# Gate scans behind the gate weight's split, and value-window copies spread between attention units, in a hybrid encoder layer

## The chip, the cores and the metric

The kernel runs on one core of a Trainium2 chip. The metric is the device time of one execution in microseconds (us). Differences are stated in us and, where it helps, in per cent of the 1353.88 us median of the kernel before.

## What is computed

One encoder layer over 1024 tokens of width 1024, with 16 learned meta tokens put in front. A normalised input `u` is multiplied by one wide weight `w_in`; the columns of the product feed two groups of heads:

```
u = rmsnorm(h);  q_na, k_na, v_na, q_gl, k_gl, v_gl, g_gl, z_gl = split(u @ w_in)
o_na = rmsnorm(neighbourhood_attention(q_na, k_na, v_na, rpb))
la   = log_sigmoid(z @ up + bias) / 16            (gates, forward and backward)
b    = cumsum(la) within chunks of 64             (the "gate scan")
o_gl = rmsnorm(gla(q*exp(b), k*exp(-b), v)) * silu(g_gl)
h    = h + rmsnorm([o_na, o_gl] @ w_o);  h = h + rmsnorm(conv_gated_ffn(rmsnorm(h)))
```

The 8 attention heads look at a window of 8 rows by 16 columns of a 64-wide token grid, plus the meta tokens. The 4 gated-linear-attention (GLA) heads work in chunks of 64.

## The kernel before

Every float32 product is done as three products of split operands: a weight or activation is copied to a rounded high part `hi` on ACT (L148) and its remainder `lo = src - hi` is computed on DVE (L149). The program text is unrolled; at build time a planner simulates the engines and fixes the order of the instructions on each engine. Its priority is the order of the program text (moved forward inside `high_priority`), and an instruction is placed when the simulation finds it ready. Two calls constrain it. `keep_in_program_order(x)` adds an edge (order of issue only) from `x` to the instruction that precedes it in the text on the same engine; `issue_after(ins)` adds such an edge to `ins` from everything that the block traces on that engine.

**First place of the change: gates.** The gate stage handles 4 heads. `gla_gate(hd)` makes gate logits on PE, `|x|` on ACT (L307) and `min(x,0)` on DVE (L308), then exp and log on ACT (L309, L310), a subtraction on POOL (L311), and two scans on DVE (L312 for the forward half, L313 for the backward half) into `C`. `gla_exp(hd)` copies the chunk ends (POOL, L322 to L325), subtracts (POOL, L326 and L327), and takes three exponentials on ACT: of the difference into `A` (L334), of `-C` into a new buffer `B` (L335) and of `C` in place (L336). The tag `gb` of the buffers `B` has two slots, shared by the gate stage's `gt_b` (which the scans read) and by `gla_exp`'s `B`; the latter pair stays in use until `gla_head` runs, so the `B` of heads 0 and 1 can be placed only when the scans of heads 2 and 3 have read theirs. `pv` (L188 to L190) are nine row blocks of the GLA value projection, evacuated at L193. `proj_g(blk)` multiplies `u` by gate weight block `wg0` or `wg1` (L175 to L177, weights stationary), per head in three token parts of 272, 256 and 512 columns, whose PSUM tiles come from a tag with two buffers (`ps_a`, shared with `pv` and all later projections), and evacuates each with a Silu on ACT (L290). The first Silu is pinned:

```python
x = nc.scalar.activation(mgl[:, hd, ...], ps[:, s0:n], AF.Silu)      # L290
if hd == 0 and ci == 0:
    tc.keep_in_program_order(x)
```

In the kernel before, the text runs: `gla_gate(3)`, `gla_exp(0)`, `gla_exp(1)`, `pv(5, 9)`, `proj_g(0)`, and `proj_g(0)` itself begins with the load and split of `wg0`. So the ACT instruction that precedes the first Silu in the text is the `hi` copy of `wg0`'s second half. Exp/log and Silu belong to different activation tables; a switch is an ACT_TABLE_LOAD.

**Second place: value windows.** The attention values are projected in two blocks of 256 columns (`half` 0 and 1) into `v_d` in DRAM. `v_windows(half)` then copies, DRAM to DRAM on the SP queue, for each of four row blocks `b` and four column windows `q`, the rows that unit (b, half) will need into `vw_d[b, half, q]`: one DMA (L498) for b = 0 and 1, and two (L500 for the meta row, L501 for the rest) for b = 2 and 3; 24 DMAs a half. For `half` 1 this stands in the step list in `v 1`, between the attention units `na b p` (row block b, pair p of heads).

```python
T1 = ("qk 3", "na 0 0", "na 0 1", "v 1", "na 1 0", "na 1 1")
T2 = ("na 0 2", "wg 1", "na 0 3", "gains", "w15", "nn 0", "wg 2", "na 1 2", ...)
```

A unit loads its query `qr` (L624), its keys `kt0` and `kt1` (L639, or L641 and L642 for b of 2 and 3) and, when p is even, four value windows `vt` (L557, four slots in all, each freed by the last value product L694 of the units that used it). Its score products are L670 to L672, the probabilities' transposes L688, their copy to SBUF on ACT L690 (`pT`). Between T1 and T2 the eight row blocks of `w_o` are loaded (`wor`, L734, three slots) and split into `wo` (L148, L149); `wg i`, `wn i` and `w15` are products with `w_o` (L763 to L767, L780); `gains` loads two gain rows (L862) and `post_a` loads `xr` (L811).

Of the kernel before, what the change touches and what calls it, by code (L numbers as in the profile page):

```python
# [8 lines left out]
F32 = mybir.dt.float32  # L9
# [4 lines left out]
ALU = mybir.AluOpType  # L14
# [16 lines left out]
QC0 = (0, 8, 24, 40)  # L31
QW = (24, 32, 32, 24)
QT = (0, 1, 1, 2)
BR0 = (0, 0, 4, 8)
BNR = (8, 11, 11, 8)
# [15 lines left out]
def _mask_offsets():  # L51
# [18 lines left out]
)  # L70
T1 = ("qk 3", "na 0 0", "na 0 1", "v 1", "na 1 0", "na 1 1")
T2 = (
# [3 lines left out]
)  # L76
T3 = (
    "wt 6", "wn 7", "ul 1", "ul 2", "wg 8", "ul 3", "ul 4", "ul 5", "u15", "wn 8", "fr", "wt 7",
# [4 lines left out]
def kernel(ctx: ExitStack, tc: tile.TileContext, a: dict):  # L83
    nc = tc.nc
# [10 lines left out]
    vw_d = {  # L95
        (b, half, q): dram.tile([(BNR[b] + 1) * QW[q], 256], F32, name=f"vw_d{b}_{half}_{q}")
        for b in range(4)
        for half in range(2)
        for q in range(4)
    }  # L100
# [36 lines left out]
    def col(i):  # L137
        return vec[:, i : i + 1]

    def rstd_small(pool, ss, n, width, name):  # L140
        v = pool.tile([P, 1], F32, tag="rs_v", name=f"{name}_v", bufs=6)
        r = pool.tile([P, 1], F32, tag="rs_r", name=f"{name}_r", bufs=6)
        nc.vector.tensor_scalar(v[:n], ss, 1.0 / width, EPS, ALU.mult, ALU.add)  # L143
        nc.gpsimd.tensor_tensor(r[:n], v[:n], nhalf[:n], ALU.pow)  # L144
        return r

    def split(hi, lo, src):
        nc.scalar.copy(hi, src)  # L148
        nc.vector.tensor_tensor(lo, src, hi.bitcast(F32), ALU.subtract)  # L149

    t1 = ExitStack()
    up = t1.enter_context(tc.tile_pool(name="up", bufs=1))
# [4 lines left out]
    def load_w(src, w, name):  # L157
        hs, ls = [], []
        for kh in range(2):
            raw = wp.tile([P, 4, 256], F32, tag="wr", name=f"{name}_r{kh}", bufs=2)  # L160
            nc.sync.dma_start(raw[:, :, :w], src[:, 4 * kh : 4 * kh + 4, :])
            hi = wp.tile([P, 4, 256], F32R, tag="wh", name=f"{name}_h{kh}")
            lo = wp.tile([P, 4, 256], F32R, tag="wl", name=f"{name}_l{kh}")
            split(hi[:, :, :w], lo[:, :, :w], raw[:, :, :w])
            hs.append(hi)
            ls.append(lo)
        return hs, ls
# [40 lines left out]
    with tc.tile_pool(name="p1", bufs=2) as p1:  # L208
        g_pre = p1.tile([P, D], F32, name="g_pre", bufs=1)
        nc.sync.dma_start(g_pre, a["norm_mix_pre"].broadcast_to([P, D]))  # L210
        for i in range(9):
            n = NM if i == 0 else P
# [6 lines left out]
            r = rstd_small(p1, ss[:n], n, D, f"rs1_{i}")  # L219
# [10 lines left out]
            if i == 1:  # L230
                vw = load_w(a["w_in_b"][4], 256, "wvg0")
# [7 lines left out]
    def gla_tile(tag, name, bufs):  # L239
        return gp.tile([P, L], F32, tag=tag, name=name, bufs=bufs)  # L240
# [39 lines left out]
        nc.gpsimd.memset(t, 0.0)  # L280
        asb.append(t)

    def proj_g(blk):
        hs, ls = load_w(a["w_in_b"][blk], 256, f"wg{blk}")
        for j in range(2):
            hd = 2 * blk + j

            def evac_g(ci, t0, n, ps, hd=hd):
                s0 = 15 if ci == 0 else 0
                x = nc.scalar.activation(mgl[:, hd, t0 + s0 - 15 : t0 + n - 15], ps[:, s0:n], AF.Silu)  # L290
                if hd == 0 and ci == 0:
                    tc.keep_in_program_order(x)

            proj_t(hs, ls, j * P, P, evac_g, f"pg{hd}")

    gA, gB, gC, gdec = {}, {}, {}, {}

    def gla_gate(hd):
        A = gla_tile("ga", f"gt_a{hd}", 2)
        B = gla_tile("gb", f"gt_b{hd}", 2)  # L300
        C = gp.tile([P, L], F32, name=f"gc{hd}")
        gbias = col(VEC_GB + hd)
        for ci, (t0, n) in enumerate(TOK):
            ps = (ps_s, ps_b, ps_c)[ci](f"gate{hd}_{ci}")
            mm(ps[:, :n], gwh[:, hd, :], zT[:, t0 : t0 + n], start=True, stop=False)
            mm(ps[:, :n], gwl[:64, hd, :], zT[:64, t0 : t0 + n], start=False, stop=True)
            nc.scalar.activation(A[:, t0 : t0 + n], ps[:, :n], AF.Abs, bias=gbias)  # L307
            nc.vector.tensor_scalar(B[:, t0 : t0 + n], ps[:, :n], gbias, 0.0, ALU.add, ALU.min)  # L308
        nc.scalar.activation(A, A, AF.Exp, scale=-1.0)  # L309
        nc.scalar.activation(A, A, AF.Ln, bias=1.0)  # L310
        nc.gpsimd.tensor_sub(B, B, A)  # L311
        nc.vector.tensor_tensor_scan(C[:64], d0[:64], B[:64], 0.0, ALU.mult, ALU.add)  # L312
        nc.vector.tensor_tensor_scan(C[64:, ::-1], d0[64:, ::-1], B[64:, ::-1], 0.0, ALU.mult, ALU.add)  # L313
        gC[hd] = C

    def gla_exp(hd):
        A = gla_tile("ga", f"ga{hd}", 2)
        B = gla_tile("gb", f"gb{hd}", 2)
        C = gC[hd]
        Cx = C[:, NM:].rearrange("p (n c) -> p n c", c=64)  # L320
        bl = gp.tile([P, 17], F32, tag="bl", name=f"bl{hd}", bufs=2)
        nc.gpsimd.tensor_copy(bl[:64, 0:1], C[:64, NM - 1 : NM])  # L322
        nc.gpsimd.tensor_copy(bl[64:, 0:1], C[64:, 0:1])
        nc.gpsimd.tensor_copy(bl[:64, 1:17], Cx[:64, :, 63])
        nc.gpsimd.tensor_copy(bl[64:, 1:17], Cx[64:, :, 0])  # L325
        nc.gpsimd.tensor_sub(A[:, :NM], bl[:, 0:1].broadcast_to([P, NM]), C[:, :NM])  # L326
        nc.gpsimd.tensor_sub(  # L327
            A[:, NM:].rearrange("p (n c) -> p n c", c=64),
            bl[:, 1:17].unsqueeze(2).broadcast_to([P, NCH, 64]),
            Cx,  # L330
        )
        dec = gp.tile([P, 17], F32, tag="dec", name=f"dec{hd}", bufs=2)
        nc.scalar.activation(dec, bl, AF.Exp, scale=0.0625)
        nc.scalar.activation(A, A, AF.Exp, scale=0.0625)  # L334
        nc.scalar.activation(B, C, AF.Exp, scale=-0.0625)  # L335
        nc.scalar.activation(C, C, AF.Exp, scale=0.0625)  # L336
        gA[hd], gB[hd], gdec[hd] = A, B, dec
# [143 lines left out]
    def na_v(half, after=None):  # L481
        hs, ls = load_w(a["w_in_b"][10 + half], 256, f"wvn{half}")
        for i in range(9):
            proj_v1(i, hs, ls, v_d, 256 * half, f"pvn{half}", True)
            if i == 0 and after is not None:
                after()
        v_windows(half)

    def v_windows(half):
        vv = v_d[:, 256 * half : 256 * half + 256].rearrange("(r c) d -> r c d", c=64)  # L490
        for b in range(4):
            nr, r0 = BNR[b], BR0[b]
            for q in range(4):
                w = QW[q]
                cols = slice(QC0[q], QC0[q] + w)
                dst = vw_d[b, half, q].rearrange("(r c) d -> r c d", c=w)
                if r0 == 0:
                    nc.sync.dma_start(dst, vv[: nr + 1, cols, :])  # L498
                else:
                    nc.sync.dma_start(dst[0], vv[0, cols, :])  # L500
                    nc.sync.dma_start(dst[1:], vv[r0 + 1 : r0 + 1 + nr, cols, :])  # L501

    hs, ls = load_w(a["w_in_b"][5], 256, "wvg1")
    pv = lambda i0, i1: [proj_v1(i, hs, ls, vg_d, 256, "pvg1") for i in range(i0, i1)]
    gla_gate(0)
    gla_gate(1)
    pv(0, 3)
    gla_gate(2)
    pv(3, 5)
    gla_gate(3)  # L510
    gla_exp(0)
    gla_exp(1)
    pv(5, 9)
    proj_g(0)
    proj_g(1)
    tc.keep_in_program_order(nc.scalar.preload_act_table_set("natural_log_exp_and_others"))
    steps = {"gqk": proj_qk, "head": gla_head, "exp": gla_exp, "qk": na_qk}

# [213 lines left out]
    for k in (4, 5, 6, 7, 0, 1, 2, 3):  # L732
# [3 lines left out]
        hi, lo = hl[:, :D], hl[:, D : 2 * D]  # L736
# [120 lines left out]
    gains = {}  # L857
# [8 lines left out]
    def nn(b):  # L866
        ms = ps_c(f"nms{b}")
        for t in range(2):
            mm(ms[:, t : t + 1], ssq[b][:, t * P : t * P + P], ones[:, :1], start=True, stop=True)
            rna[2 * b + t + 1] = rstd_small(pp3, ms[:, t : t + 1], P, 512, f"rna{b}_{t}")  # L870

    def step2(name):
        op, *n = name.split()
        n = [int(x) for x in n]
        if op == "na":
            na_step(*n)
        elif op == "nn":
            nn(*n)
        elif op == "gains":
            load_gains()  # L880
        elif op == "w15":
            wo_15()
        else:
            st = sts.setdefault(n[0] if n else 0, {})
            if op == "wg":
                wo_mm(n[0], st, 0)
            elif op == "wn":
                wo_mm(n[0], st, 1)
                post_a(n[0], st)
            elif op == "wt":  # L890
                post_b(n[0], st)
            elif op == "ul":
                u2_load(n[0])
            elif op == "u15":
                nc.gpsimd.tensor_copy(u2["a"][:, :, :1], u15)
            elif op == "fr":
                prep(0)
# [517 lines left out]
```

## Time and profile before

| | us |
|---|---|
| runs (median of 3) | 1353.88 (1353.38 to 1354.87) |
| the profiled execution, own time | 1352.37 |
| its span in the profile | 1350.7 |
| PE busy in the span | 1268.2 (94%) |
| DVE, ACT, POOL busy | 914.0, 619.3, 429.7 |

Mean granted TensorE clock over the span: 0.973 of full speed. The 1.67 us between the execution's own time and its span lie outside the traced instructions. "Idle" in a row is the time that the engine sat before an instruction, and the arrow names what ended that time; SPq rows are the issue of DMAs by the SP queue, not their transfer.

### The profile page before, as it was taken

What the parts mean: (1) busy time and instruction counts of PE and PEld (TensorE: products, weight loads), DVE (VectorE), ACT (ScalarE), POOL (GpSimd) and SP (SyncE); (2) the same over time, 40 slices, a digit from 0 to 9 for tenths busy, and PEclk for the clock granted to TensorE, in tenths of its full rate; (3) what the DMA queues carried; (4) which work ended last, traced back from release to release, by engine and by line L of the source; (5) the groups of instructions that cost most, each with busy time, mean ns of one, the idle gap of its engine ahead of it and who ended that gap; (6) DMA issues with size and microseconds to landing.
All of it is one profiled execution on the core that took longest, in us unless ns stands there. A gap on an engine that the chain in (4) does not pass through costs nothing.

```text
span 1350.7 us, 23581 instructions
## 1 busy us (share of the span) xinstructions
PE 1268.2 (94%) x9048; PEld 1139.0 (84%) x9050; DVE 914.0 (68%) x1453; ACT 619.3 (46%) x1198; POOL 429.7 (32%) x401
## 2 busy tenths in 40 slices
PE   7979999999997899998779999999999999999997
PEld 6869888988886587776779999999999998888876
DVE  6491365254544577865979898898888978555556
ACT  5443544152332555656544444344443444545542
POOL 1260001000021154432556565765657633000001
PEclk9989999999988889999889999999999999999999
DMA  6311132351187545842134434444344456866735
GB/s 204 119 38 50 34 93 84 110 177 64 51 270 225 208 132 197 278 137 94 40 117 149 142 124 164 167 154 143 124 164 159 154 173 228 303 198 207 247 125 187
DMA packets 117137, 203.74 MB, mean 151 GB/s; under 512 B 18080, under 2 KB 51200, under 8 KB 117024
## 3 DMA queue, kind: packets, MB, share of 16 engines
q1 hardware_dynamic: 117024, 202.24, 44.6%
q8 instruction: 71, 1.16, 0.4%
q14 instruction: 42, 0.34, 0.1%
HBM read 145.64 MB, written 66.19 MB: 157 GB/s over the span
## 4 chain that ended last, share of the span: by engine, by line
PE 63%; DVE 18%; DMA 6%; ACT 5%; issue 5%; POOL 1%; SPq 1%; DVEq 0%; ACTq 0%; POOLq 0%
DVE bl L924 5%; PE bank L1202 4%; PE bank L1201 4%; PE bank L1200 4%; PE q_r L966 3%; PE q_r L967 3%; PE q_r L968 3%; PE ops L694 2%; PE pna L175 2%; PE pna L176 2%; PE pna L177 2%; DVE g L1015 2%; PE pp L688 2%; PE wo L766 2%; PE wo L767 2%
## 5 line engine op out<-in xcount | busy, mean ns | idle before, releaser
L966 PE MATMUL q_r<-ah,bh 128*128 128x258 f32 x504 | 145.4, 288 | 14.9 <-ACT c L1079 14.9
L967 PE MATMUL q_r<-al,bh 128*128 128x258 f32 x504 | 144.3, 286 | 0.0
L968 PE MATMUL q_r<-ah,bl 128*128 128x258 f32 x504 | 143.9, 285 | 0.0
L966 PEld LDWEIGHTS q_r<-ah,bh 128*128 128x128 f32 x504 | 97.1, 193 | 17.2 <-ACT c L1079 17.1
L149 DVE TENSOR_TENSOR ol<-r,oh 128x512 fp32r<-128x512 f32 x116 | 74.6, 688 | 46.0 <-ACT oh L148 46.0
L1200 PE MATMUL bank<-oh,oh 128*128 128x512 f32 x264 | 102.9, 390 | 2.2 <-DVE c L1266 2.2
L1201 PE MATMUL bank<-oh,ol 128*128 128x512 f32 x264 | 102.7, 389 | 0.0
L1202 PE MATMUL bank<-ol,oh 128*128 128x512 f32 x264 | 102.2, 389 | 0.0
L966 PE MATMUL q_z<-ah,bh 128*128 128x258 f32 x336 | 95.4, 284 | 6.3 <-DVE y L1015 4.9
L1025 ACT ACTIVATE g<-g 128x512 f32<-128x512 f32 (+1 forms) x46 | 28.2, 614 | 157.0 <-DVE g L1015 156.9
L967 PEld LDWEIGHTS q_r<-al,bh 128*128 128x128 f32 x504 | 97.0, 193 | 0.0
L968 PEld LDWEIGHTS q_r<-ah,bl 128*128 128x128 f32 x504 | 97.0, 192 | 0.0
L967 PE MATMUL q_z<-al,bh 128*128 128x258 f32 x336 | 95.2, 283 | 0.0
L968 PE MATMUL q_z<-ah,bl 128*128 128x258 f32 x336 | 95.0, 283 | 0.0
L148 ACT CAST oh<-r 128x512 fp32r<-128x512 f32 x116 | 65.6, 619 | 50.2 <-PE bank L1201 40.0
L924 DVE TENSOR_TENSOR bl<-bt,bh 128x512 fp32r<-128x512 f32 x84 | 85.2, 1015 | 3.5 <-ACT bh L922 3.5
L924 DVE TENSOR_TENSOR bl<-fr,bh 128x512 fp32r<-128x512 f32 x67 | 64.5, 966 | 17.4 <-ACT bh L922 17.2
L1011 ACT ACTIVATE g<-c,vec 128x512 f32<-128x512 f32 (+1 forms) x46 | 36.6, 795 | 75.2 <-DVE c L1140 40.8
L966 PEld LDWEIGHTS q_z<-ah,bh 128*128 128x128 f32 x336 | 63.9, 190 | 6.7 <-issue 5.1
L144 POOL TENSOR_TENSOR rsc_r<-rsc_v,nhalf 128x1 f32<-128x1 f32 x8 | 5.8, 725 | 197.5 <-DVE rsc_v L143 197.5
L1014 DVE SCALAR_TENSOR_TENSOR g<-c,vec,g 128x512 f32<-128x512 f32 (+1 forms) x46 | 53.5, 1164 | 17.1 <-ACT g L1011 17.1
L1026 DVE TENSOR_TENSOR y<-y,g 128x512 f32<-128x512 f32 (+1 forms) x46 | 54.9, 1194 | 13.4 <-ACT g L1025 13.3
(388 smaller groups left out, 4257.9 us busy)
## 6 DMA issues: line engine op xcount, KB each, us to landing
fr<-in_w_ffn_in_dram SPq DMA_DIRECT2D x44, 512.0 KB
y_d<-y SPq DMA_DIRECT2D x44, 256.0 KB
w<-in_w_ffn_out_dram SPq DMA_DIRECT2D x22, 512.0 KB
t_d<-w SPq DMA_DIRECT2D x22, 512.0 KB
s_d<-y SPq DMA_DIRECT2D x44, 256.0 KB
r<-s_d SPq DMA_DIRECT2D x44, 256.0 KB
r<-t_d SPq DMA_DIRECT2D x44, 256.0 KB
r<-y_d SPq DMA_DIRECT2D x25, 256.0 KB
```

The costliest lines, as they stand in the source:

```text
L148: nc.scalar.copy(hi, src)
L149: nc.vector.tensor_tensor(lo, src, hi.bitcast(F32), ALU.subtract)
L924: nc.vector.tensor_tensor(lo, src, hi.bitcast(F32), ALU.subtract)
L966: mm(ps, w[0][:, k, :], A[0][:, k, c], start=(first and k == 0), stop=False, skip_group_check=True)
L967: mm(ps, w[0][:, k, :], A[1][:, k, c], start=False, stop=False, skip_group_check=True)
L968: mm(ps, w[1][:, k, :], A[0][:, k, c], start=False, stop=(last and k == 3), skip_group_check=True)
L1011: nc.scalar.activation(dst, tap(1), AF.Identity, bias=col(VEC_CB + ch), scale=col(VEC_CONV + 2 * NFC + ch))
L1014: nc.vector.scalar_tensor_tensor(dst, tap(0), col(VEC_CONV + ch), dst, ALU.mult, ALU.add)
L1026: nc.vector.tensor_mul(val, val, g)
L1200: mm(ps, A[0][:, tk], B[0], start=first, stop=False, skip_group_check=True)
L1201: mm(ps, A[1][:, tk], B[0], start=False, stop=False, skip_group_check=True)
L1202: mm(ps, A[0][:, tk], B[1], start=False, stop=last, skip_group_check=True)
```

## The change

The scans of heads 2 and 3 are taken out of `gla_gate` into `gla_scan` and stand in the text behind the load and split of `wg0`, with an order edge to the `lo` subtraction of `wg0`'s second half (`lo_last[0]`); `gla_exp(0)` and `gla_exp(1)` move behind them, and so behind `pv(5, 9)`. The load of `wg0` moves from inside `proj_g` to before the scans. The copies of value half 1 are split: b = 0 stays in `v 1`; b = 1, 2 and 3 become the steps `vw 1`, `vw 2`, `vw 3` behind `na 0 2`, `na 0 3` and `na 1 2`, each with an order edge to the last SP instruction that the text has at that point (the last DMA of that unit).

```diff
 T2 = (
-    "na 0 2", "wg 1", "na 0 3", "gains", "w15", "nn 0", "wg 2", "na 1 2", "wn 1", "na 1 3", "nn 1", "wt 1", "wn 2",
...
+    "na 0 2", "vw 1", "wg 1", "na 0 3", "vw 2", "gains", "w15", "nn 0", "wg 2", "na 1 2", "vw 3", "wn 1", "na 1 3",
...
     def split(hi, lo, src):
         nc.scalar.copy(hi, src)
-        nc.vector.tensor_tensor(lo, src, hi.bitcast(F32), ALU.subtract)
+        lo_last[0] = nc.vector.tensor_tensor(lo, src, hi.bitcast(F32), ALU.subtract).ins
...
-    def proj_g(blk):
-        hs, ls = load_w(a["w_in_b"][blk], 256, f"wg{blk}")
+    def proj_g(blk, w):
+        hs, ls = w
...
         nc.gpsimd.tensor_sub(B, B, A)
+        gB[hd], gC[hd] = B, C
+        if hd < 2:
+            gla_scan(hd)
+
+    def gla_scan(hd):
+        B, C = gB[hd], gC[hd]
         nc.vector.tensor_tensor_scan(C[:64], d0[:64], B[:64], 0.0, ALU.mult, ALU.add)
         nc.vector.tensor_tensor_scan(C[64:, ::-1], d0[64:, ::-1], B[64:, ::-1], 0.0, ALU.mult, ALU.add)
-        gC[hd] = C
...
-        v_windows(half)
-
-    def v_windows(half):
+        for b in range(1 if half else 4):
+            v_windows(half, b)
+
+    def v_windows(half, b):
...
     gla_gate(3)
+    pv(5, 9)
+    w = load_w(a["w_in_b"][0], 256, "wg0")
+    with tc.issue_after(lo_last[0]):
+        gla_scan(2)
+        gla_scan(3)
     gla_exp(0)
     gla_exp(1)
-    pv(5, 9)
-    proj_g(0)
-    proj_g(1)
+    proj_g(0, w)
+    proj_g(1, load_w(a["w_in_b"][1], 256, "wg1"))
...
+        elif op == "vw":
+            with tc.issue_after(last(mybir.EngineType.SP)):
+                v_windows(1, *n)
```

## Rows read from the trace of the kernel before

**Rows 1.** The page's first line: the span of the profiled execution.

```profile
span 1350.7 us, 23581 instructions
```

**Rows 2.** Stretches: length, busy PE PEld DVE ACT POOL (instructions), PEclk, DMA share, GB/s.

```profile
120.00:360.00 240.00, 239.65 (x1710) 215.52 (x1711) 109.97 (x237) 88.83 (x164) 8.47 (x14) 1.00 0.28 88
444.00:620.00 176.00, 172.39 (x1370) 132.25 (x1371) 121.90 (x331) 100.53 (x276) 68.21 (x115) 0.96 0.53 171
```

**Rows 3.** PE's waits, 60 to 150 us: total, times, longest.

```profile
PE pg L177 <- DVE wg_l L149: 7.7, 1, 7.7
```

**Rows 4.** DVE in order of time, 85 to 104 us: start, us, what.

```profile
85.90 4.48 DVE L312 TENSOR_TENSOR_SCAN gc<-d,gt_b 64x1040 f32<-64x1040 bf16 x1
90.42 4.02 DVE L313 TENSOR_TENSOR_SCAN gc<-d,gt_b 64x1040 f32<-64x1040 bf16 x1
94.47 2.92 DVE L149 TENSOR_TENSOR wg_l<-wg_r,wg_h 128x1024 fp32r<-128x1024 f32 x1
97.32 0.74 DVE L193 COPY pvg_s<-pvg 128x256 f32<-128x256 f32 x2
...
100.36 2.32 DVE L313 TENSOR_TENSOR_SCAN gc<-d,gt_b 64x1040 f32<-64x1040 bf16 x1
```

**Rows 5.** POOL in order of time, 85 to 93 us.

```profile
85.77 2.43 POOL L311 TENSOR_TENSOR gt_b<-gt_b,gt_a 128x1040 f32<-128x1040 f32 x1
88.17 2.23 POOL L326 TENSOR_TENSOR ga<-bl,gc 128x16 f32<-128x16 f32 x1
90.36 1.90 POOL L327 TENSOR_TENSOR ga<-bl,gc 128x1024 f32<-128x1024 f32 x1
```

**Rows 6.** ACT in order of time, 86 to 108 us.

```profile
86.54 1.05 ACT L148 CAST wg_h<-wg_r 128x1024 fp32r<-128x1024 f32 x1 [4.30 <-PE pvg L189]
...
97.54 1.28 ACT L290 ACT_TABLE_LOAD   x1
100.12 0.39 ACT L290 ACTIVATE mgl<-pg 128x257 f32<-128x257 f32 x1 [1.29 <-PE pg L177]
...
106.87 1.07 ACT L336 ACTIVATE gc<-gc 128x1040 f32<-128x1040 f32 x1
```

**Rows 7.** PE in order of time, 89 to 110 us.

```profile
97.45 0.59 PE L177 MATMUL pg<-uh,wg_l 128*128 128x272 f32 x1 [7.66 <-DVE wg_l L149]
...
103.81 0.39 PE L175 MATMUL pg<-uh,wg_h 128*128 128x512 f32 x1
...
109.39 0.29 PE L175 MATMUL pg<-uh,wg_h 128*128 128x272 f32 x1
```

**Rows 8.** Two stretches behind a PE stall, columns as in rows 2.

```profile
97.40:103.80 6.40, 6.35 (x34) 6.35 (x35) 6.34 (x5) 5.06 (x6) 3.93 (x7) 0.61 0.44 125
443.90:449.50 5.60, 5.60 (x36) 3.25 (x37) 4.51 (x12) 5.60 (x14) 1.49 (x2) 0.50 0.93 372
```

**Rows 9.** PE's waits, 360 to 470 us: total, times, longest.

```profile
PE ops L694 <- ACT pT L690: 9.0, 1, 9.0
```

**Rows 10.** The SP queue's DMA issues, 417 to 437 us.

```profile
417.88 3.11 SPq L498 DMA_DIRECT2D vw_d<-v_d  x4
...
422.76 0.68 SPq L734 DMA_DIRECT2D wor<-in_w_o_dram  x1
426.86 7.79 SPq L501 DMA_DIRECT2D vw_d<-v_d  x8
434.76 2.15 SPq L734 DMA_DIRECT2D wor<-in_w_o_dram  x3
```

**Rows 11.** ACT, the copy of the fifth wo block and what follows it.

```profile
442.41 1.04 ACT L148 CAST wo<-wor 128x1024 fp32r<-128x1024 f32 x1 [11.76 <-DMA wor<-in_w_o_dram]
443.36 0.85 ACT L690 COPY pT<-pp 96x384 f32<-96x384 f32 x2
```

**Rows 12.** The SP queue's DMA issues, 488 to 489 us.

```profile
488.24 0.32 SPq L557 DMA_DIRECT2D vt<-vw_d  x1
488.61 0.46 SPq L642 DMA_DIRECT2D kt<-kT_d  x1
```

**Rows 13.** PE, last score product of the first window that uses those keys.

```profile
495.77 0.30 PE L672 MATMUL sp<-kt,qbh 128*128 128x288 f32 x1
```

More of the change, by code (lines that the diff above doesn't have):

```diff
@@ L145, in rstd_small, with last @@
         return r
+    lo_last = [None]
+    def last(engine):
+        traced = nc.cur_bb.bb.instructions
+        return next(i for i in reversed(traced) if i.engine == engine)
     def split(hi, lo, src):
         nc.scalar.copy(hi, src)
-        nc.vector.tensor_tensor(lo, src, hi.bitcast(F32), ALU.subtract)
+        lo_last[0] = nc.vector.tensor_tensor(lo, src, hi.bitcast(F32), ALU.subtract).ins
     t1 = ExitStack()
@@ L486, in na_v @@
                 after()
-        v_windows(half)
-    def v_windows(half):
+        for b in range(1 if half else 4):
+            v_windows(half, b)
+    def v_windows(half, b):
         vv = v_d[:, 256 * half : 256 * half + 256].rearrange("(r c) d -> r c d", c=64)
[L491 to L501, printed above, removed]
+        nr, r0 = BNR[b], BR0[b]
+        for q in range(4):
+            w = QW[q]
+            cols = slice(QC0[q], QC0[q] + w)
+            dst = vw_d[b, half, q].rearrange("(r c) d -> r c d", c=w)
+            if r0 == 0:
+                nc.sync.dma_start(dst, vv[: nr + 1, cols, :])
+            else:
+                nc.sync.dma_start(dst[0], vv[0, cols, :])
+                nc.sync.dma_start(dst[1:], vv[r0 + 1 : r0 + 1 + nr, cols, :])
     hs, ls = load_w(a["w_in_b"][5], 256, "wvg1")
```

4 rows, old and new, of the table T2 are left out of this document.

## The prediction

> **What bounds the kernel now.** I read the page's header first for the span, 1350.7 us [rows 1]; the profiled execution's own time is 1352.37, and the median of the runs lies 1.51 above that, so I work out a difference against the profiled execution and add it to 1353.88. About 0.2% of this, 2.7 us, is what a measurement of this kernel can tell from no change. Then I read the stretches. Between 120 and 360 us PE is busy 239.65 of 240 us, and from 444 to 620 it is busy 172.39 of 176 [rows 2]: what is won or lost ahead of these stretches reaches the end, since PE has no idle time there that could take it up. So I ask PE's waits, by stretch, and find two that the change is near. The first is 7.7 us for the `lo` half of the gate weight at 97 us [rows 3, 7]. The second is 9.0 us for a `pT` copy at about 435 to 444 us [rows 9]. Both are followed by matmuls at the lower clock: from 97.4 to 103.8 the granted clock averages 0.61, from 443.9 to 449.5 it is 0.50 [rows 8]. At 0.50 a stretch takes twice its work, so the first costs (1 - 0.61) x 6.4 = 2.5 us of PE time and the second 0.50 x 5.6 = 2.8 us.
>
> **Part 1, the gate scans: what is removed.** Read DVE downward [rows 4]. The second scan pair in view (head 2) starts at 85.90 and ends at 94.44, and only then comes the `lo` subtraction that PE waits for. The scans are long because POOL has turns in between: the POOL subtraction ends at 88.20, and a 16-element POOL step that starts at 88.17 takes 2.23 us and ends at 90.40, just when the first scan does [rows 4, 5]. One waits for the other; a scan alone takes 2.32, and the 2.92 us of the `lo` subtraction hold its wait for POOL too. With the order edge the `lo` subtraction goes first. Its input is ready at 86.54 + 1.05 = 87.6 [rows 6], POOL's turn ends at 88.2, and at 1.2 us (2.92 less the 1.7 us wait) it ends at 89.4. PE wants it at 97.45 - 7.66 = 89.8. So the 7.7 us wait and its 2.5 us of clock are gone there: up to -10.2 us.
>
> **Part 1: what it adds.** The moved load of `wg0` changes who stands before the first Silu in the text. Before, it was the `hi` copy of `wg0`; now it is the last exponential of `gla_exp(1)`, L336. The pin in `evac_g` therefore puts the first Silu behind L336 of head 1 on ACT. In the trace of before the first Silu runs at 100.12 and that L336 only at 106.87 [rows 6]: the pin reverses them. Head 1's L335 and L336 can't be early either, because their `B` takes a slot that the scan of head 3 must have read. PE has two `ps_a` buffers, so it can fill the 272 and the 256 columns but must have the first Silu before the 512 columns.
>
> Now in time. PE at 89.8 has 10 matmuls of 0.125 us and 24 of 0.118 us left in the first two products: it stands still from 93.7. DVE and POOL do the same work as before in another order (lo, four scan halves, POOL's turns), so the scan of head 3 still ends at 100.36 + 2.32 = 102.7 [rows 4]. Then L335 and L336 at 1.07 each (the second starts 0.1 early), a table load of 1.28 and a Silu of 0.39 [rows 6]: 102.7 + 2.0 + 1.3 + 0.4 + 0.1 = 106.5. Before, the 512-column product ran from 103.81 to 109.39, 5.58 us at full clock [rows 7]. Now it starts at 106.5, after 12.8 us of idle, and I charge it the 2.5 us that the stall of before cost: it ends at 106.5 + 5.6 + 2.5 = 114.6, that is **+5.2 us**. Both ends: if the pin or the slot doesn't bind, -10.2; if the two `pvg_s` copies (0.74) and more POOL steps also fall into the scans' chain, +7. I take +5.2, since each term is a row of this very work. Nothing hides it: PE is full for the 240 us behind it [rows 2].
>
> The switches of the activation table between Silu and exp fall from five to one, since all exponentials now come first. At 1.28 us each [rows 6] that is 5.1 us of ACT, which PE doesn't wait for, so I cost it at nothing. The Trainium skill (ScalarE: Activation LUTs, What ACT_TABLE_LOAD costs) has a drain of about 1.38 us with every switch, 2.66 us in all. The row shows 1.28 alone; by the page the first Silu, and the total, would come 1.4 us later.
>
> **Part 2, the value windows: what is removed.** Follow the 9.0 us back. `pT` stands on ACT behind the copy of the fifth `wo` block, which begins at 442.41 after 11.76 us of waiting for its DMA [rows 11]. That DMA was issued with two others at 434.76, behind 7.79 us in which SP issued eight window copies [rows 10], and it landed 7.7 us after its issue because those copies (1.3 MB for b = 2, 0.9 MB for b = 3, read and written) were in the rings before it. All eight are moved, as are the four of b = 1 at 417.88 and the eight meta rows. Now the fifth block can be issued next to the fourth at 423.4; with a landing like the fourth's or even the fifth's 7.7 us it is there by 431, its copy is done by 432.2, and `pT` follows at 432.4, when its transposes end. PE would ask for it at about 434.9. So the wait goes, and with it the clock: -9.0 - 2.8 = **-11.8 us**. Next late is nothing in sight: PE waits under 4 us in all in the 176 us that follow [rows 2]. If the gain rows and `xr` (2 MB, ready earlier) were put ahead of the fifth block, it would be some 3 to 5 us later and up to 3 of the 9.0 would stay.
>
> **Part 2: what is added.** Twenty DMAs, some 15 us of SP issue at 0.78 to 0.97 each [rows 10], come between the loads of the units, and 3.7 MB of copies go into the rings in front of them. `vw 1` and `vw 2` push loads that the units fetch one unit ahead; I cost them at nothing, and if that lead is gone they cost 0.8 us for each DMA in front. `vw 3` is tighter. Its anchor is the `vt` load at 488.24, and right behind that stands the last key load of unit (2, 0) at 488.61 [rows 12], used by PE at 495.77 [rows 13]. Eight copies ahead of it move its issue to at most 496.4, and with a landing of at most 7.7 us, as the `wor` load had behind such copies, it is there at 504: a wait of 0 (if the planner keeps that load in front) to 8.3 us, plus 2.8 us for the clock behind it. I take +2.5: half of the eight are 32 KB or less, and the planner has other matmuls to put there.
>
> **Sum.** +5.2 - 11.8 + 2.5 = -4.1 us; 1353.88 - 4.1 = 1349.8 us.
>
> **Rivals.** (a) *Both stalls go.* If the first Silu isn't held, part 1 gives -10.2 in full: -10.2 - 11.8 + 2.5 = -19.5, 1334.4 us. Against it stands the text: the pin takes whatever ACT instruction was traced last, and that is now L336. Chance 0.10. (b) *The moved copies become the new wait.* Place: the rings and the SP queue in front of the units' loads from 450 to 500 us. Price: the 8.3 + 2.8 us of the key load above instead of 2.5, and one more wait of some 3 us where `vt` loads of row block 1 must now wait for copies issued one unit earlier: +5.2 - 11.8 + 14.1 = +7.5, 1361 us. It decides from 9.3 us of new waits on, where the total passes +2.7. For it: a load behind copies took 7.7 us. Against it: PE has matmuls with `w_o` between the units, and most loads are a unit ahead. Chance 0.15. The Trainium skill (DMA: Bandwidth & Descriptors, Queues, rings and completion order) says that each DMA engine takes the descriptors of a ring in the order in which they were queued. By that rule a key load can't pass copies issued before it, and the late `wor` load agrees. (c) *Half of (b)*: new waits of 4 to 9 us cancel the net, -2.7 to +2.7, about 1353.9. This is also where the change does only part of what it says: the wait for `wo` partly stays. Chance 0.25.
>
> **How the numbers follow.** The forecast, new waits of 0 to 4 us, has 0.50 and its own range of 1346 to 1351. With (a) at 0.10 faster than 0.2% has 0.60, within 0.2% 0.25, slower 0.15. The range runs from 1341, which leaves out (a) in full but takes in a gate part that costs nothing, to 1358, which takes in (c) and the lower half of (b).
>
> **What would show it.** Right: PE's wait for `wg_l` is gone; PE idles some 13 us before the first 512-column product and its releaser is the first Silu, which stands behind all L336 of heads 0 and 1; one table load instead of five; `wor` issues close together near 423 us plus the shift, and no 9 us wait for `pT`. Wrong: a Silu between the exponentials; a `pT` wait that stays; PE waits above 4 us for `kt` or `vt` behind `vw 3`.

## The result, and the profile after

The changed kernel takes 1341.16 us (median of 4 runs, 1338.45 to 1341.93) against 1354.38 for the kernel before on the same chip: a ratio of 0.9899, 95% interval 0.9887 to 0.9912, or -13.7 us. The forecast was -4.1. In the experiments below a difference is always (ratio - 1) x 1354 us against the kernel before on the same chip.

The profiled run has this span, 14.0 us under [rows 1]:

```profile
span 1336.7 us, 23582 instructions
```

**Two places moved, in opposite directions.** The last `pvn` product, 300 us behind the gates, ends at 417.4 before and at 421.4 after (417.6 and 421.1 in a second profile of each): the gate part costs 4 us, and the full stretch in between carries it on. From there to the end of the last attention unit PE runs the same 1408 matmuls in both kernels. The stretches view (length, busy PE PEld DVE ACT POOL with instructions, granted clock, DMA share, GB/s) has for the kernel before

```profile
417.42:616.58 199.16, 183.05 (x1408) 139.99 (x1407) 132.61 (x357) 108.84 (x290) 70.75 (x119) 0.93 0.57 186
```

and for the changed kernel

```profile
421.40:603.60 182.20, 175.87 (x1408) 137.21 (x1406) 129.04 (x357) 109.64 (x290) 77.71 (x119) 0.97 0.63 204
```

Read the first two columns: 17 us less, of which PE's idle time (length less busy) fell from 16.1 to 6.3. The clock column tells the next part. The stretches at the lower level (1.2 of 2.4 GHz) are, before,

```profile
423.20:430.00 6.80, 5.32 (x12) 3.74 (x13) 3.87 (x12) 2.00 (x5) 0.00 (x0) 0.50 0.86 304
436.90:450.50 13.60, 6.62 (x39) 3.52 (x40) 5.92 (x12) 7.95 (x18) 1.86 (x2) 0.50 0.92 357
484.60:491.50 6.90, 6.90 (x36) 5.81 (x34) 5.30 (x15) 4.85 (x14) 4.26 (x8) 0.51 0.71 215
```

and after

```profile
427.20:434.10 6.90, 5.33 (x13) 4.17 (x14) 5.10 (x13) 2.11 (x4) 0.77 (x1) 0.51 1.00 370
471.60:475.00 3.40, 3.40 (x14) 3.28 (x15) 0.73 (x3) 1.26 (x4) 0.00 (x0) 0.50 0.47 131
```

Half of PE's busy time in each, summed, gives 9.4 us lost before and 4.4 after. What is left, 173.7 against 171.5, is called the rest here: neither idle nor lost to the clock. What follows the last unit takes 734.1 us before and 733.1 after.

**The gates.** PE's waits from 60 to 150 us (total, times, longest), to be set against [rows 3]:

```profile
PE pg L181 <- DVE pvg_s L199: 5.2, 1, 5.2
PE pg L181 <- ACT mgl L296: 4.0, 1, 4.0
```

The wait for `wg_l` is gone, and two others stand there, 9.2 us in place of 7.7. Between 85 and 150 us the lower clock costs 3.9 us (2.4 and 1.5 in the two profiles of before; half of PE's busy time, as above). DVE in order of time (start, us, what), which answers to [rows 4]:

```profile
87.98 1.67 DVE L155 TENSOR_TENSOR wg_l<-wg_r,wg_h 128x1024 fp32r<-128x1024 f32 x1 [1.63 <-ACT wg_h L154]
89.57 2.33 DVE L324 TENSOR_TENSOR_SCAN gc<-d,gt_b 64x1040 f32<-64x1040 bf16 x1
91.93 3.85 DVE L325 TENSOR_TENSOR_SCAN gc<-d,gt_b 64x1040 f32<-64x1040 bf16 x1
95.81 0.76 DVE L199 COPY pvg_s<-pvg 128x256 f32<-128x256 f32 x2
96.60 3.23 DVE L324 TENSOR_TENSOR_SCAN gc<-d,gt_b 64x1040 f32<-64x1040 bf16 x1
```

The `lo` subtraction goes first, as the order edge says. But the two `pvg_s` copies, which free the PSUM buffer that PE's second gate product needs, now stand behind head 2's scans, at 95.81. PE, whose gaps are

```profile
96.62 0.58 PE L181 MATMUL pg<-uh,wg_h 128*128 128x256 f32 x1 [5.21 <-DVE pvg_s L199]
...
105.03 0.80 PE L181 MATMUL pg<-uh,wg_h 128*128 128x512 f32 x1 [4.02 <-ACT mgl L296]
```

does one product of 24 matmuls, waits 5.2, does the second, waits 4.0. The second wait is read on ACT, against [rows 6]:

```profile
102.21 1.07 ACT L346 ACTIVATE gb<-gc 128x1040 f32<-128x1040 f32 x1 [2.50 <-DVE gc L325]
103.30 1.28 ACT L296 ACT_TABLE_LOAD   x1
104.60 0.39 ACT L296 ACTIVATE mgl<-pg 128x256 f32<-128x256 f32 x1
105.00 1.28 ACT L347 ACT_TABLE_LOAD   x1
106.29 1.07 ACT L347 ACTIVATE gc<-gc 128x1040 f32<-128x1040 f32 x1
107.37 1.28 ACT L296 ACT_TABLE_LOAD   x1
108.66 0.39 ACT L296 ACTIVATE mgl<-pg 128x257 f32<-128x257 f32 x1
```

The pinned Silu (the 257 columns, part 0) does wait behind the last exponential of head 1 and runs at 108.66, 8.5 us later than in [rows 6]. The Silu of part 1 has no pin; it goes in front at 104.60 and frees PE.

**The value windows.** The SP queue's issues, against [rows 10]:

```profile
418.12 4.05 SPq L206 DMA_DIRECT2D v_d<-pvn_s  x2
...
424.35 0.33 SPq L749 DMA_DIRECT2D wor<-in_w_o_dram  x1
...
426.17 0.65 SPq L749 DMA_DIRECT2D wor<-in_w_o_dram  x1
...
427.49 0.38 SPq L749 DMA_DIRECT2D wor<-in_w_o_dram  x1
...
432.06 5.42 SPq L749 DMA_DIRECT2D wor<-in_w_o_dram  x2
```

and ACT's copy of the fifth block with the `pT` behind it, against [rows 11]:

```profile
434.80 1.05 ACT L154 CAST wo<-wor 128x1024 fp32r<-128x1024 f32 x1 [4.87 <-DMA wor<-in_w_o_dram]
435.76 0.47 ACT L705 COPY pT<-pp 96x384 f32<-96x384 f32 x1
```

No copy stands between the loads of `w_o` any more, and `pT` is there at 435.8 instead of 443.4, although everything up to here runs 4 us later. The load of the fifth block is issued at 426.17 instead of 434.76. It is no quicker: from its issue to its copy on ACT go 8.6 us, against 7.7 before. What the change wins here is the time of issue. PE's waits for DMA from 360 to 470 us, where [rows 9] had 9.0 for `pT`:

```profile
PE sp L685 <- DMA kt<-kT_d: 2.5, 1, 2.5
...
PE ops L709 <- DMA vt<-vw_d: 0.7, 1, 0.7
```

The first of these stands near 388 us, as one of 2.2 did before. Behind `vw 3`, where the forecast had set a wait for keys, the last copy is issued at 484.57 and the key loads follow:

```profile
484.57 0.65 SPq L512 DMA_DIRECT2D vw_d<-v_d  x1
485.32 0.41 SPq L656 DMA_DIRECT2D kt<-kT_d  x1
```

and PE waits for none of them: it is busy for all of 478 to 510 us.

### The profile page after: what moved, and what is told of

The parts are those of the page before. It is cut to its first block, busy times and chain, and to the rows that moved or that the text cites. A ratio compares the mean times of both kernels' runs of the same rounds, so it can differ in the third digit from the quotient of the medians.

```text
span 1336.7 us, 23582 instructions
## 1 busy us (share of the span) xinstructions
PE 1264.2 (95%) x9050; PEld 1138.6 (85%) x9050; DVE 907.8 (68%) x1453; ACT 618.3 (46%) x1196; POOL 436.0 (33%) x401
## 4 chain that ended last, share of the span: by engine, by line
PE 62%; DVE 16%; issue 5%; DMA 4%; ACT 4%; POOL 1%; SPq 0%; DVEq 0%; ACTq 0%; POOLq 0%
DVE bl L942 5%; PE bank L1218 4%; PE bank L1219 4%; PE bank L1220 4%; PE q_r L984 3%; PE q_r L985 3%; PE q_r L986 3%; PE pna L181 2%; PE ops L709 2%; PE pna L182 2%; PE pna L183 2%; PE wo L781 2%; PE wo L782 2%; PE wo L778 2%; PE pp L703 2%
## 5 line engine op out<-in xcount | busy, mean ns | idle before, releaser
L154 ACT CAST oh<-r 128x512 fp32r<-128x512 f32 x116 | 65.5, 619 | 50.4 <-PE bank L1219 40.9
L942 DVE TENSOR_TENSOR bl<-fr,bh 128x512 fp32r<-128x512 f32 x67 | 65.2, 977 | 16.4 <-ACT bh L940 16.3
L1044 DVE TENSOR_TENSOR y<-y,g 128x512 f32<-128x512 f32 (+1 forms) x46 | 57.1, 1242 | 13.4 <-ACT g L1043 13.3
L986 PEld LDWEIGHTS q_z<-ah,bl 128*128 128x128 f32 x336 | 63.8, 190 | 0.0
```

The source lines that it names most:

```text
L986: mm(ps, w[1][:, k, :], A[0][:, k, c], start=False, stop=(last and k == 3), skip_group_check=True)
L1044: nc.vector.tensor_mul(val, val, g)
```

## The experiments

Line numbers differ by a few between the kernels, since the edits move lines.

**1. The gates alone** (the steps and loops of the windows as before).

```diff
-T2 = ("na 0 2", "vw 1", "wg 1", "na 0 3", "vw 2", "gains", ...
+T2 = ("na 0 2", "wg 1", "na 0 3", "gains", ...
-        for b in range(1 if half else 4):
+        for b in range(4):
```

> The gate part of the change alone, all copies of value half 1 in their old place. Theory (the gate part costs, the window part brings all of the gain and more): in the changed kernel the third gate product starts 1.2 us later than before and runs at the lower clock, and the first key projection starts at 147.1 instead of 143.5 us, so this kernel is 3 to 5 us slower than before, about 1358. Rival (the gate part pays, since the wait for the lo half of the weight is gone): 5 to 10 us faster than before.

Measured: 1357.79 us, ratio 1.0031 (1.0016 to 1.0046), +4.2 us. PE's waits, first from 60 to 150, then from 360 to 470 us:

```profile
PE pg L181 <- DVE pvg_s L199: 5.2, 1, 5.2
PE pg L181 <- ACT mgl L296: 3.5, 1, 3.5
...
PE ops L709 <- ACT pT L705: 8.0, 1, 8.0
```

The gate half of the change is a loss, by the two waits just read and the clock behind them, and the stall for `pT` stays, at 8.0.

**2. The windows alone** (the kernel before, with the steps `vw` and the split of `v_windows`).

```diff
+T2 = ("na 0 2", "vw 1", "wg 1", "na 0 3", "vw 2", "gains", ...
+        for b in range(1 if half else 4):
+            v_windows(half, b)
...
+        elif op == "vw":
+            with tc.issue_after(last(mybir.EngineType.SP)):
+                v_windows(1, *n)
```

> The window part of the change alone, gates as before. Theory: the gate part cost about 3.6 us, so without it this kernel is faster than the whole change by 3 to 5 us: about 1337, 17 us under the kernel before. Rival (the two parts help each other, or the gate part pays): not faster than the whole change, 1341 or more.

Measured: 1338.02, ratio 0.989 (0.9869 to 0.9911), -14.9 us. The old gate wait is there again:

```profile
PE pg L181 <- DVE wg_l L153: 7.6, 1, 7.6
```

and no wait for `pT`. The two halves add to +4.2 - 14.9 = -10.7 against -13.7 for the whole, which agrees within the intervals (2 us to each side for the gates, 3 for the windows, 2 for the whole). That this kernel is 3 to 5 us faster than the whole change isn't shown: the 1.2 us between the two lie within the intervals.

**3. The change without the first Silu's pin.**

```diff
-                x = nc.scalar.activation(mgl[...], ps[:, s0:n], AF.Silu)
-                if hd == 0 and ci == 0:
-                    tc.keep_in_program_order(x)
+                nc.scalar.activation(mgl[...], ps[:, s0:n], AF.Silu)
```

> The changed kernel without the pin of the first Silu. Theory (the pin makes the planner take the second part's Silu first, but the wait of 4.0 us for a Silu comes from ACT's own order, with head 1's exponential of -C waiting for the scan of head 3): with the pin gone a Silu can go ahead of it, as before at 100 us, and the 4.0 us wait and its clock go, 4 to 6 us faster than the changed kernel. Rival (ACT's order is the same without the pin): within 1 us of the changed kernel.

Measured: 1338.63, ratio 0.9893 (0.9871 to 0.9915), -14.5 us. ACT in order of time:

```profile
94.94 1.07 ACT L343 ACTIVATE ga<-ga 128x1040 f32<-128x1040 f32 x1 [4.27 <-POOL ga L336]
96.03 1.28 ACT L296 ACT_TABLE_LOAD   x1
97.33 0.39 ACT L296 ACTIVATE mgl<-pg 128x257 f32<-128x257 f32 x1
```

The first Silu slips in between the exponentials at 97.33. The wait of 4.0 is gone, as expected; in the place of the 5.2 PE still waits, now for this Silu:

```profile
PE pg L181 <- ACT mgl L296: 5.0, 1, 5.0
```

From the first to the last `pg` product (L181, start to start) the stage takes 52.0 us (89.5 to 141.5), against 58.2 in the change and 55.0 before. So the pin is worth 6 us of this stage. The expected 4 to 6 us aren't in the median, which is 0.8 below the change's: the attention stage takes them back in its rest (experiments 10 and 11).

**4. Without the pin (the edit of 3), and with the copies ahead of the scans.**

```diff
     pv(5, 9)
+    copied = last(mybir.EngineType.DVE)
     w = load_w(a["w_in_b"][0], 256, "wg0")
-    with tc.issue_after(lo_last[0]):
+    with tc.issue_after(lo_last[0]), tc.issue_after(copied):
```

> As the kernel without the pin, and with the moved scans also ordered behind the last evacuation copy of the GLA value projection. Theory: the 5.2 us that PE waits for that copy, which stands behind head 2's scans on DVE, goes too, with its clock: 5 to 8 us faster than the kernel without the pin, 9 to 13 us faster than the changed kernel, about 1330. Rival (the wait for a Silu takes its place): no faster than the kernel without the pin.

Measured: 1334.75, ratio 0.985 (0.9834 to 0.9866), -20.3 us: **the fastest kernel of this study**, faster than before and than the change. Its gate stage takes 50.4 us, and PE's only long wait there is

```profile
PE pg L181 <- ACT mgl L296: 4.7, 3, 2.3
```

in three short pieces, and the clock stays at its full level from 85 to 150 us. The last `pvn` product ends at 413.6: the gates turn from +4 into a gain of 4 once the two things that the change put in PE's way are taken out again. The expectation was 9 to 13 us under the change and some 1330 in all; it is 6.6 under. Of the 5.8 against experiment 3, 1.6 are in the gate stage; the largest part lies in the attention stage, whose rest is 4.9 and 4.3 us less than in the two profiles without the pin.

**5. All three groups of copies directly behind the loads of `w_o`.**

```diff
-T2 = ("na 0 2", "vw 1", "wg 1", "na 0 3", "vw 2", "gains", ..., "na 1 2", "vw 3", ...
+T2 = ("vw 1", "vw 2", "vw 3", "na 0 2", "wg 1", "na 0 3", "gains", ..., "na 1 2", ...
```

> The changed kernel with its three groups of copies put one after the other directly behind the last load of w_o, not between the attention units. All else as in the change, so the reference is the change's -13.7 us against the kernel before. Theory A (all that the window part gains is that the loads of w_o no longer stand behind copies; where the copies go after that is worth little): -11 to -16 us, no wait of PE for pT above 2 us. Rival B (the spreading between the units is a gain of its own, because loads of the units then don't stand behind 20 copies): some 15 us of SP issue and 3.7 MB come ahead of the value and key loads of units (1, p), PE waits 4 us or more for vt or kt, and only -3 to -9 us are left.

Measured: 1348.38, ratio 0.9955 (0.994 to 0.9971), -6.1 us. The stall for `pT` is gone, and yet half of the gain is missing: rival B's size. Of its mechanism, long waits for keys and values, only one such wait is new (1.9 us for `kt`). The stretch of the 1408 matmuls takes 190.4 us, 8 more than in the change: 4 of idle, most of it in small pieces, 2 of clock, 2 of the rest. Where the copies go does matter; by which wait is only partly shown.

**6. Every moved copy issued twice.**

```diff
             with tc.issue_after(last(mybir.EngineType.SP)):
                 v_windows(1, *n)
+                v_windows(1, *n)
```

> The changed kernel with each of the three moved groups of copies issued twice, 40 DMAs where there were 20 and 7.4 MB where there were 3.7; the second time writes the same values. Reference: the change's -13.7 us. Theory A (the moved copies lie in slack of SP and of the rings): 0 to +2 us against the change, so -11.5 to -14 us. Rival C (the moved copies have a price of their own, the +2.5 of my sum or more, which something else in the window part hid): doubling it adds at least the same again, +2.5 to +8 us against the change, -11 to -5.5 us, with a wait for kt or vt behind the second or third group.

Measured: 1346.88, ratio 0.994 (0.9918 to 0.9962), -8.1 us, 5.6 less than the change: rival C's size. From 478 to 515 us a query load is late for ACT,

```profile
ACT qbh L647 <- DMA qr<-qT_d: 4.6, 1, 4.6
```

and PE stands idle 1.1 us in 477 to 483 with the lower clock around it. One set of copies fits between the units; a second doesn't. That the late query load is the copies' doing fits the order of issue, but isn't shown by itself.

**7 and 8. Only row block 1 moved; only row blocks 2 and 3 moved.**

```diff
-T2 = ("na 0 2", "vw 1", "wg 1", "na 0 3", "vw 2", "gains", ..., "na 1 2", "vw 3", ...
+T2 = ("na 0 2", "vw 1", "wg 1", "na 0 3", "gains", ..., "na 1 2", ...
-        for b in range(1 if half else 4):
+        for b in (0, 2, 3) if half else range(4):
```

and

```diff
-T2 = ("na 0 2", "vw 1", "wg 1", "na 0 3", "vw 2", "gains", ..., "na 1 2", "vw 3", ...
+T2 = ("na 0 2", "wg 1", "na 0 3", "vw 2", "gains", ..., "na 1 2", "vw 3", ...
-        for b in range(1 if half else 4):
+        for b in range(2 if half else 4):
```

> The changed kernel with only the copies of row block 1 moved (four, 0.64 MB); those of blocks 2 and 3 (sixteen, eight of them the large ones) are issued in front of w_o as before. By my steps the eight large copies in front of the fifth block of w_o are what holds it. Theory A: PE's wait for pT stays at 6 to 9 us, the window part gives 0 to -3, and with the gates' +4 the total is +1 to +4 us. Rival D (any copies moved give a share of the gain in step with their bytes or their issues): a fifth of -17, with +4 about +0.5 us, and half the pT wait gone.

> The changed kernel with only the copies of row blocks 2 and 3 moved; the four of block 1 stay in front of w_o, 4 us of SP issue. Theory A: the fifth block of w_o is issued next to the fourth, lands before PE needs it, no wait for pT above 2 us: -11 to -14 us in total. Rival D (in step with issues): the four copies keep a fifth of the gain back, 3 to 4 us, with a pT wait of 3 us or so: -9 to -10.5 us. If the fourth piece of the surplus (clock and small gaps, some 7 us beyond my -9.3) hangs on the order that follows from w_o being early at all, it is here too.

Measured: 1352.13, ratio 0.999 (0.9976 to 1.0004), -1.4 us, with block 1 moved; 1349.01, ratio 0.9965 (0.9946 to 0.9984), -4.7 us, with blocks 2 and 3. Less the gates' +4.2 the halves bring -5.6 and -8.9, the whole -17.9. Neither theory has both: A is off in 7 by 2.4 us and in 8 by 6, D is 1.9 off in 7 and 4 in 8. (The four copies of block 1 move 1.3 MB by the trace, 384 or 288 KB each, and not the 0.64 MB of the expectation.) The eight ACT copies of `w_o` show the common cause (duration min/median/max, first and last start), before, after, in 7 and in 8:

```profile
L148 ACT CAST wo<-wor x8: 1044/1046/1053, 418.2 to 456.0; 128x1024 fp32r<-128x1024 f32 x8
```

```profile
L154 ACT CAST wo<-wor x8: 1044/1047/1058, 421.7 to 441.7; 128x1024 fp32r<-128x1024 f32 x8
```

```profile
L154 ACT CAST wo<-wor x8: 1030/1046/1057, 420.7 to 455.8; 128x1024 fp32r<-128x1024 f32 x8
```

```profile
L154 ACT CAST wo<-wor x8: 1044/1049/1059, 422.2 to 446.3; 128x1024 fp32r<-128x1024 f32 x8
```

With blocks 2 and 3 left in front, `w_o` is as late as before (455.8), and PE waits for it in another place,

```profile
PE wo L778 <- ACT wo L154: 5.6, 1, 5.6
```

With the four copies of block 1 left in front it is 4.6 us later than in the change, and PE waits

```profile
PE sp L685 <- DMA wor<-in_w_o_dram: 2.9, 1, 2.9
```

and then runs at the lower clock from 441 to 452, which costs 5.1 us: more than the wait. The Trainium skill (DMA: Bandwidth & Descriptors, Queues, rings and completion order) has the descriptors of a ring taken in the order of queueing. In 7 a load of `w_o` issued behind eight copies is copied 7.9 us after its issue, which agrees; but in the change, behind a gain row and `xr`, it is 8.6, so these runs don't show that copies hold a load any longer than other loads do.

**9. The copies at their new places, without the order edges.**

```diff
-            with tc.issue_after(last(mybir.EngineType.SP)):
-                v_windows(1, *n)
+            v_windows(1, *n)
```

> The changed kernel without the three order edges that put each group of copies behind SP's last instruction in the text: the copies stand at the same places of the list of steps, but the planner may issue them as early as their input allows. Theory A (w_o early is what counts, and the planner takes the copies for what they are in the text): within 3 us of the change, -11 to -16 us. Rival E (without the edge the copies drift back in front of w_o, since their input has long been ready): most of the gain is lost, -2 to +4 us, with the pT wait back at 6 to 9 us.

Measured: 1359.79, ratio 1.003 (1.0013 to 1.0047), +4.1 us, just what the gates alone cost. The SP queue shows why:

```profile
430.71 1.61 SPq L512 DMA_DIRECT2D vw_d<-v_d  x2
432.44 0.46 SPq L749 DMA_DIRECT2D wor<-in_w_o_dram  x1
...
438.17 1.98 SPq L512 DMA_DIRECT2D vw_d<-v_d  x2
440.81 0.83 SPq L749 DMA_DIRECT2D wor<-in_w_o_dram  x1
```

The copies, ready early, are put between the loads of `w_o` again, and PE has a wait of 7.4 us that ends at 445, now behind DVE:

```profile
PE sp L685 <- DVE mn L690: 9.3, 3, 7.4
```

The moved places in the text do nothing by themselves; the edges do it.

**10 to 12. The change, the kernel without the pin, and the kernel before, each a second time**, no edit.

> The changed kernel itself, a second time, for a second profile. From the end of the last pvn product to the end of the last attention unit the same 1408 matmuls took 199.2 us before, 182.3 in the change's first profile, and 183.8, 190.9 and 187.3 in three experiments with the same window part. Theory F (the 8.6 us between 182.3 and 190.9 lie in the order that the planner gives to PE, which is another in each kernel): the second profile has 181 to 184 again, 6 to 7 us of idle and 4 to 5 of clock. Rival G (they are what one run differs from another): it lies anywhere from 182 to 191. Time: 1339 to 1343, ratio 0.989 to 0.991.

> The changed kernel without the first Silu's pin, a second time, for a second profile: its first had 190.9 us from the end of the last pvn product to the end of the last attention unit, 178.3 of it neither idle nor lost to the clock, and was the slowest of its runs. Theory F (order): 189 to 192 again. Rival G (run to run): 182 to 188, with 171 to 174 us that are neither idle nor clock.

> The kernel before, a second time, for a second profile of the same stretch: 199.2 us in the first, of which 16.1 idle and 9.4 lost to the clock. Theory F: 197.5 to 201 with 15 to 17 idle and 8 to 10 of clock. Rival G: it comes out 4 us or more apart, as run differs from run, and the surplus of the window part is then not to be told from chance by profiles.

Measured: the change 1338.95, ratio 0.9887 (0.9871 to 0.9902), -15.3 us; without the pin 1340.35, ratio 0.9902 (0.9882 to 0.9921), -13.3 us; the kernel before 1355.18 in its one run. The stretch of the 1408 matmuls, from all the profiles (us; the clock's loss worked out as above, the rest what is neither idle nor clock; the last column is explained below):

```
                        length   idle   clock   rest   steps
before                   199.2   16.1     9.4   173.7      39
before, again            197.6   16.7     6.2   174.6      39
gates alone              199.1   15.3     6.3   177.5      55
no edge                  199.5   15.2     7.7   176.6      43
block 1 moved            193.9   13.1     7.1   173.8      41
blocks 2 and 3 moved     192.7   10.0     9.6   173.1      30
behind w_o               190.4   10.5     6.0   174.0      28
copies twice             188.7    8.1     7.8   172.8      34
no pin                   190.9    8.3     4.3   178.3      60
no pin, again            188.4    6.2     4.5   177.7      60
no pin, copies first     187.3    7.8     6.1   173.4      37
windows alone            183.8    7.1     4.5   172.2      27
the change               182.3    6.4     4.4   171.5      31
the change, again        182.0    7.3     3.0   171.8      31
```

Idle time and clock move by up to 3 us from run to run of one kernel; the rest stays within 1. Theory F holds for the lengths of the change (182.3 and 182.0) and of the kernel before, and for the rest without the pin (178.3 and 177.7); the second length without the pin, 188.4, lies below F's 189 to 192, and the second clock losses, 3.0 and 6.2, below F's 4 to 5 and 8 to 10. So the 6 us of rest between the change and the kernel without the pin belong to the kernel and not to the run; what differs in this stage is the order that the planner chose.

One thing in that order can be counted, the steps between `w_o` products and value products (`ops`) in the last column. At full clock a `w_o` product between two others is followed after 0.23 us (medians, here and in the next sentence). The last one ahead of a value product is followed after 0.33, the first one behind a value product after 0.34. From a value product to a `w_o` product it is 0.15, where from one value product to the next it is 0.034 in the mean. So the way to the value products costs 0.09 us, the way back 0.12 + 0.11. The change goes there 19 times and back 12, the kernel without the pin 33 and 27. That is 14 x 0.09 + 15 x 0.23 = 4.7 us, three quarters of the 6; the remainder is open. Over all fourteen profiles the three with 55 or 60 steps have the longest rest; between 27 and 43 steps the two go together only roughly (28 with 174.0, 34 with 172.8).

## Why the prediction was right or wrong

The sum was +5.2 - 11.8 + 2.5 = -4.1; the result is -13.7, near the fast end of the range. The sign held, and so did the removal of both waits that were named; the step that failed is the size of the window part, put at -9.3 (-11.8 + 2.5). By the means of the two profiles of each kernel it came to -16.3, the gate part to +3.7, and what runs behind the last unit to -2.7 (736.2 against 733.5 us, where the two profiles of before alone lie 4 apart). These add to -15.2, 1.5 beyond the medians, which is within the spread of two profiles.

**Gates, +5.2: size right within 1.5, path only half right.** The predicted removal came: `lo` first, 1.67 us long where I had 1.2, and no wait for `wg_l`. So did the price of the pin: a Silu behind the last exponential. What failed is the sentence that PE fills the 272 and the 256 columns and must then have the first Silu. It could not fill the 256, since the two `pvg_s` copies went into the chain of scans, which I had only as the upper end; and it needed not the first Silu but any, and the unpinned one of part 1 came 4 us ahead of the pinned one. So there are two stalls of 5.2 and 4.0 instead of one of 13, and three table loads where I forecast one. Stalls and clock together came to 9.2 + 3.9 = 13.1 us, not 12.8 + 2.5 = 15.3, so that the total came out near is in part luck. (PE's 34 matmuls end at 93.9 by the numbers given, not at 93.7; nothing in the sum hangs on it.) My own sign of being wrong, a Silu between the exponentials, is there. Experiments 3 and 4 price the two causes in this stage at 6.2 us for the pin and, with the pin gone, 1.6 for the copies.

**No drain.** The table load ends at 103.30 + 1.28 = 104.58 and the Silu starts at 104.60. The Trainium skill (ScalarE: Activation LUTs, What ACT_TABLE_LOAD costs) has 1.38 us of drain in every switch; none is seen here, and taking the row's 1.28 was right.

**Windows, the removal of -9.0: right.** The fifth block of `w_o` is copied at 434.8 and `pT` follows at 435.8, later than my 432.4 since `v_d` stores, gain rows and `xr` went ahead and everything is 4 us late, but in time. My reason was half right: the eight copies held the issue of that block, and the landing of 7.7 us, which I put down to them too, is 8.6 without them. That the copies of blocks 2 and 3 hold `w_o` is shown by experiment 7. I had costed the four copies of block 1 in front of it at nothing of their own; experiment 8 shows that they alone keep 9 us of the gain back.

**Windows, the new waits of +2.5: wrong, and the first part of the miss.** They were charged for a key load behind `vw 3`, out of 0 to 8.3 us and 2.8 of clock. The copies were issued from 479.76, 8.5 us ahead of where [rows 12] put their anchor, since the stage itself ran earlier by then, and PE met no wait: the term measured nothing. Idle time fell by 9.6 (16.4 to 6.8) where I had -9.0 + 2.5. The slack isn't large: a second set of copies cost 5.6 us.

**Windows, the clock of -2.8: right in kind, under in size.** Only the dip behind the `pT` stall was counted. The kernel before has three low stretches between 417 and 617 and the change has two or one; the loss fell from 7.8 to 3.7, -4.1, with a spread of 3 between two profiles of the kernel before.

**Not in the sum at all: the order of PE's work.** The planner rewrites PE's order when DMAs move in the text. In the change the rest is 2.5 us less than before (174.2 to 171.7), with 31 steps between `w_o` and value products against 39: 4 x 0.09 + 4 x 0.23 = 1.3 of the 2.5. In the kernel without the pin, with the same window part and 60 steps, it is 4 us more than before. No row of the trace of before could have told this; a range has to allow for it.

Together: -3.1 of waits, -1.3 of clock, -2.5 of order and -1.5 of gates make 8.4 of the 9.6 us between forecast and result. The clock's share is no larger than its spread and so is the least certain. Rivals (b) and (c) are out for the change as it stands. Rival (a) failed as stated, since the pin does bind. Its price is wrong too: experiment 3, where the first Silu isn't held, has -14.5 and -13.3, not -19.5. Experiment 4 comes near that number with -20.3, but its gate part gains 4 us and not 10.2, so the nearness is chance.

## What to carry to other kernels

A DMA that nobody needs soon belongs, with an explicit order edge, behind the loads that somebody needs now: at the same place in the text without the edge it gained nothing. When an instruction is pinned to its predecessor in the text, look at who the predecessor is after a move, and which unpinned sibling may overtake it. Before believing a difference of a few us in a stage that a planner orders, profile the same kernel twice and compare the idle time, the clock and the rest apart.

## What was not expected of the hardware

What stands behind a wait can cost more than the wait: in experiment 8 one of 2.9 us is followed by a stretch at the lower clock, 441 to 452 us, that costs 5.1. In experiment 4 three waits of up to 2.3 us in the gate stage are followed by none.

PE's time for the same matmuls, neither idle nor at the lower clock, ranged from 171.5 to 178.3 us from kernel to kernel, with their order as what differs. Between the change and the kernel without the pin three quarters of it are, as counted above, the price of going between a 512-column `w_o` product (128*128) and a 64-column value product (128*64): 0.09 us there and 0.23 back, over staying with either. PE of the changed kernel in order of time shows one such place:

```profile
499.82 0.75 PE L709 MATMUL ops<-pT,vt 128*64 128x64 f32 x20
500.50 0.50 PE L778 MATMUL wo<-wo,mh 128*128 128x512 f32 x1
500.84 0.39 PE L781 MATMUL wo<-wo,ml 128*128 128x512 f32 x1
```

The first `w_o` product behind the value products takes 0.50 us and is followed after 0.34, the next one 0.39 and 0.24. The Trainium skill (TensorEngine Tiling (Array Packing), Tiling Modes) says that a change of the tiling mode drains the engine. The value products start in pairs 0.01 us apart (499.65 and 499.66, 499.76 and 499.77), so two of 64 columns run side by side, where a `w_o` product has all 128; the rows agree in kind, but that the 0.09 and 0.23 us are this drain isn't shown by itself.
